# VectorE in program order from the first MLP on, and the state-space stage's inputs regrouped through device memory

## The chip, the cores and the metric

The kernel runs on one core of one Trainium2 chip, in one launch. The metric is device time in microseconds. Three runs of the kernel before gave 2471.07, 2461.07 and 2458.48 us, median 2461.07. Five engines work side by side: TensorE (PE; its weight loads are shown as PEld), VectorE (DVE), ScalarE (ACT), GpSimd (POOL) and SyncE (SP), which issues most of the DMAs. They meet through semaphores alone.

## The reference

A decoder trunk of two layers on one sequence of 256 tokens, model width 2048, all in float32. Layer 0 mixes tokens with stick-breaking attention, layer 1 with a diagonal state-space layer (S5) and a gated linear unit (GLU). Each layer ends with a squared-ReLU MLP of width 8192, and each of the four sub-layers is wrapped in the same way:

```
cond = silu(c)
mod = cond @ ada_w[i] + ada_b[i]              # 2048 -> 6 vectors of 2048
h = rmsnorm(x, g) * (1 + scale) + shift       # scale, shift: two of the six
x = x + gate * mixer(h)                       # gate: a third one
mlp(h)     = relu(h @ w1)**2 @ w2
s5(h):  u = h @ w_in;  state[t] = a * state[t-1] + B u[t]   (complex, 64 per group of 16 channels)
        z = gelu(C state + d * u);  y, g = split(z @ w_glu);  return y * sigmoid(g)
```

The weights are read once: 736 tiles of 512 KB for the matrix products and 384 tiles of 512 KB for `ada_w`.

## The kernel before

**Split products.** Each float32 product is made of three: a value is the sum of a rounded high part H and the remainder L, and TensorE sums L·H, H·L and H·H. A weight tile of 128x1024 therefore goes through four hands (`weights`, lines 126 to 134): SP issues its DMA into one of three buffers `w` (line 129), ScalarE copies it rounded to `wh` (line 131), VectorE subtracts to get `wl` (line 133), and TensorE multiplies with both (24 matmuls of some 256 columns on lines 160 to 162, or 12 of 512 columns on lines 146 to 148). `wh` and `wl` have three buffers each as well. So a `w` buffer is free for the next DMA when VectorE has made `wl` of it, and a `wl` buffer is free when TensorE is through with that tile.

**Ticks.** After each weight tile the program calls `tick`, which advances the products with `ada_w` by a fractional `rate` and then runs the functions that were booked for this tick with `at(delay, fn)`. The small stages of S5 and of the norms are interleaved with the weight tiles in this way.

**The products with `ada_w`.** They are sums over 2048 rows, one row block times one number per partition, on VectorE. A unit is one tile `adaw` of 128x1024 (four buffers; 32 units make one of the six vectors of a layer) and one VectorE instruction on line 356 (line 354 for the first of a sum), written straight after the load is issued. Sixteen units make one sum, for which there are three buffers (`adsums` two, `adacc` one); TensorE then adds it up over the partitions (`totals`, line 327) and frees it. The program asks for 0.42 units per weight tile in the first MLP (line 1236, from `between` on, after the first 16 tiles; 1.0 before), 0.35 in S5 (line 1248), and from the end of S5 as many as finish the last two vectors that the second MLP's input needs within 44 ticks (`pace(44, mid[-1])`, line 1122).

**Who sets the order.** `manual_schedule` on line 1190 keeps TensorE and GpSimd in the order in which the program writes their instructions. VectorE, ScalarE and SP follow a planner, which takes an instruction whenever its estimate says that it is ready, so a VectorE instruction written later can run earlier. Once planned, each engine and each DMA queue works its list strictly in order: an instruction that waits holds up all behind it.

**S5.** Eight weight groups of four tiles each give two blocks of 128 channels, 16 blocks in all, two ticks apart. For block `bi`, whose product is whole at tick T: `s5_windows` (T, VectorE then ScalarE) scales it to `u`; `s5_shuffle` (T+1) moves 32-channel strips, shifted by 0 to 3 tokens with stride 4, into other partitions with 16 matmuls against an identity (lines 1038 and 1039) and a ScalarE copy to `imc` (line 1040); `s5_operands` (T+1) and `s5_taps` (T+4) prepare operands on TensorE; `s5_states` (T+2) makes 8 matmuls with `imc` and then seven VectorE instructions (lines 1055 to 1063); `s5_outputs` (T+6) makes 44 matmuls, one VectorE instruction (line 1079) and a GELU. A float32 matmul of these shows as two records.

**The MLP.** `mlp` runs over four quarters of the 8192; `normal`, a square and `split` turn a pair of column blocks into the next operand `aH`, `aL`; `residual` adds a block to `x`, `square` adds its square to a running sum `sq`, `fold` scales it to the next sub-layer's `hH`, `hL`.

Of the kernel before, what the change touches and what calls it, by code (L numbers as in the profile page):

```python
# [8 lines left out]
F32 = mybir.dt.float32  # L9
# [7 lines left out]
P = 128  # L17
# [39 lines left out]
class Trunk:  # L57
    def __init__(self, ctx, tc, ins, out, dbg=None):
        self.ctx, self.tc, self.nc = ctx, tc, tc.nc
        self.i, self.out, self.dbg = ins, out, dbg or {}  # L60
        self.pers = ctx.enter_context(tc.tile_pool(name="pers", bufs=1))
        self.wp = ctx.enter_context(tc.tile_pool(name="wp", bufs=1))
        self.ps = ctx.enter_context(tc.tile_pool(name="ps", bufs=1, space=bass.MemoryType.PSUM))
        self.queue = []
        self.acc2 = self.wp.tile([P, 2, 512], F32, name="adacc", bufs=1)


# [67 lines left out]

    def gemm_rows(self, w2d, c0, aH, aL, k0, k1):
        nc = self.nc
        acc = self.accs()
        for t in range(k0 // 2, k1 // 2):
            r0 = 2 * t * P  # L140
            H, L = self.weights(w2d[r0:r0 + 2 * P, c0:c0 + 512].rearrange("(a p) b -> p a b", p=P), 2, 512)
            for kk in range(2):
                kb = 2 * t + kk
                for tb in range(2):
                    o, s = acc[:, tb], slice(tb * P, tb * P + P)
                    nc.tensor.matmul(o, aL(kb)[:, s], H[:, kk], start=(kb == k0), stop=False)  # L146
                    nc.tensor.matmul(o, aH(kb)[:, s], L[:, kk], start=False, stop=False)  # L147
                    nc.tensor.matmul(o, aH(kb)[:, s], H[:, kk], start=False, stop=(kb == k1 - 1))  # L148
            self.tick()
        return acc  # L150

    def cols_tile(self, acc, w2d, c0, t, aH, aL, k0=0, k1=NB):
        nc = self.nc
        r0, n = 4 * t * P, aH(0).shape[-1]
        H, L = self.weights(w2d[r0:r0 + 4 * P, c0:c0 + 256].rearrange("(a p) b -> p a b", p=P), 4, 256)
# [163 lines left out]
    def ada_dve(self, layer, groups):  # L319
        nc = self.nc  # L320
        st, rows = {}, 32 * len(groups)

        def totals(i0, accs):
            if i0 == 0:
                st["bank"] = self.ada_bank()
            for i, acc in enumerate(accs, i0):
                nc.tensor.matmul(st["bank"][32 * i:32 * i + 32], self.ones[:, 0:32], acc, start=True, stop=True)
# [13 lines left out]
        if self.sums is not None:  # L341
            for i in range(0, len(groups), 2):
                if self.turn % 3:
                    acc = self.sums.tile([P, 1024], F32, name="adsums", bufs=2)
                else:
                    acc = self.acc2.rearrange("p a b -> p (a b)")
                self.turn += 1
                accs += [acc[:, :512], acc[:, 512:]]
                vec, g = groups[i]
                for k in range(NB):  # L350
                    wt = self.ada_load(layer, vec, g, k, wide=True).rearrange("p a b -> p (a b)")
                    c = self.cond[:, k:k + 1]
                    if k == 0:
                        nc.vector.tensor_scalar(acc, wt, c, None, op0=OP.mult)
                    else:
                        nc.vector.scalar_tensor_tensor(acc, wt, c, acc, op0=OP.mult, op1=OP.add)  # L356
                    yield
            self.later(2, totals, 0, accs)
        for i, (vec, g) in enumerate(groups if not accs else []):
# [12 lines left out]
            self.later(2, totals, i, accs[i:])  # L372
        self.later(2, evict)
        self.later(3, finish)

    def ada_vec(self, layer, vec, on_pe=False):
        g = self.pending[layer, vec] = self.ada(layer, [(vec, g) for g in range(4)], on_pe)
# [61 lines left out]
    def square(self, sq, kb):  # L439
        nc = self.nc  # L440
        if kb == 0:
            nc.scalar.activation(sq, self.xT[:, kb], AF.Square)
        else:
            t = self.wp.tile([P, S], F32, name="sqt", bufs=2)
            nc.scalar.activation(t, self.xT[:, kb], AF.Square)
            nc.vector.tensor_tensor(sq, sq, t, op=OP.add)

    def new_sq(self):
        return self.wp.tile([P, S], F32, name="sqa", bufs=1)
# [52 lines left out]
    def mlp(ctx, self, layer, nxt=None, last=False, between=None):  # L502
# [9 lines left out]
        for q in range(4):  # L512
# [12 lines left out]
            for g in range(8):  # L525
# [376 lines left out]
    def s5_open(self, sp):  # L902
        g_ = self.nc.gpsimd
        self.sE = sp.tile([P, 2, 4, 4, 2, 16], F32, name="E")
        self.sCA = [sp.tile([P, 2, 4, 4, 2, 16], F32, name="CA%d" % k) for k in range(3)]
        self.sKL = [sp.tile([P, 3, 4, 2, 16], F32, name="KL%d" % k) for k in range(3)]
        self.simc = [sp.tile([P, 4, 65], F32, name="imc%d" % k) for k in range(3)]
        self.sU = [sp.tile([P, 4 + S + 1], F32, name="u%d" % k) for k in range(3)]
        self.sM = [sp.tile([P, 2, 4, 64], F32, name="M%d" % k) for k in range(2)]
        self.sP = [sp.tile([P, 224], F32, name="taps%d" % k) for k in range(2)]  # L910
        for t in [self.sE] + self.sP + self.sM + self.sCA + [u[:, 0:4] for u in self.sU]:
            g_.memset(t, 0.0)
        self.sS = {}

# [108 lines left out]
            nc.tensor.transpose(pk[:, tau * P - P:tau * P], self.sP[bi % 2][:, o:o + P], self.ident)  # L1023
        nc.scalar.activation(self.sKL[bi % 3].rearrange("p t q a e -> p (t q a e)"), pk[:, :3 * P], AF.Copy)

    def s5_windows(self, bi, acc):
        nc = self.nc
        uw = self.sU[bi % 3]
        nc.vector.tensor_tensor(uw[:, 4:], acc[:, :S + 1], self.rms, op=OP.mult)
        nc.scalar.activation(uw[:, 4:4 + S], uw[:, 4:4 + S], AF.Identity, bias=uw[:, 4 + S:])  # L1030

    def s5_shuffle(self, bi):
        nc = self.nc
        uw, imc = self.sU[bi % 3], self.simc[bi % 3]
        pi = self.mp()
        for q in range(4):
            for j in range(4):
                nc.tensor.matmul(pi[32 * j:32 * j + 32, 65 * q:65 * q + 65], self.ident[:, 32 * q:32 * q + 32],  # L1038
                                 uw[:, 4 - j:4 - j + 257:4], start=True, stop=True)
        nc.scalar.activation(imc.rearrange("p q k -> p (q k)"), pi[:, :4 * 65], AF.Copy)  # L1040

    def s5_states(self, sp, bi):
        nc, s5 = self.nc, self.s5
# [20 lines left out]

    def s5_outputs(self, sp, bi):
        nc = self.nc
        u, St = self.sU[bi % 3][:, 4:4 + S], self.sS.pop((bi, "R")).rearrange("p c (q k) -> p c q k", q=4)
# [11 lines left out]
        nc.vector.scalar_tensor_tensor(u.rearrange("p (k i) -> p i k", i=4), u.rearrange("p (k i) -> p i k", i=4),  # L1079
                                       self.dcol[:, bi:bi + 1], py[:, 0:S].rearrange("p (i k) -> p i k", i=4),  # L1080
                                       op0=OP.mult, op1=OP.add)
        nc.scalar.activation(self.z[:, bi], u, AF.Gelu_apprx_tanh)
        if not self.split_z:
            self.sdone.add(bi)
        else:
# [2 lines left out]
    def s5_mixer(self, mid):  # L1088
# [11 lines left out]
        for gi in range(8):  # L1100
# [82 lines left out]
    def run(self):  # L1183
# [100 lines left out]
```

## Time and profile before

| what | value |
|---|---|
| runs, us | 2471.07, 2461.07, 2458.48 (median 2461.07) |
| profiled execution, us | 2467.97 |
| its span, first to last instruction, us | 2466.1 |
| mean granted clock of TensorE | 0.989 |
| TensorE matmuls busy | 2365.1 us, 96% |
| VectorE busy | 1795.4 us, 73% |
| ScalarE busy | 1212.7 us, 49% |
| moved by DMA | 627.09 MB, 254 GB/s over the span |

The profile is of one execution. Busy times of matmuls overlap and their ends are modelled, so a busy TensorE can still lose time between tiles; the time that a weight tile takes, a stretch of the span divided by the tiles in it, is the steadier measure. Stages by the span's clock: attention to 455 us, first MLP to 1311, S5 and its change-over to the GLU to 1520, GLU to 1725, second MLP to the end. An engine's idle time is put down to the last semaphore that it waited for.

### The profile page before, as it was taken

How to read it: one execution, taken by the hardware profiler on the slowest of the kernel's cores; microseconds unless marked ns; L12 is line 12 of the kernel's file. 1: busy time of each engine (PE TensorE's matmuls, PEld its weight loads, DVE VectorE, ACT ScalarE, POOL GpSimd, SP SyncE). 2: the span in 40 equal slices, each digit the busy share in tenths (PEclk: the TensorE clock that was granted, in tenths of full speed). 3: DMA queues.
4: the chain of work that ended last, by engine and by line, in shares of the span. 5: the costliest groups of instructions: out<-in, count | busy, mean ns of one | idle time of the engine just before them, and what ended most of it. 6: DMA issues, size and time to landing. Idle time of an engine off the chain costs nothing.

```text
span 2466.1 us, 45235 instructions
## 1 busy us (share of the span) xinstructions
PE 2365.1 (96%) x18355; PEld 2160.4 (88%) x18355; DVE 1795.4 (73%) x2223; ACT 1212.7 (49%) x1814; POOL 316.6 (13%) x340
## 2 busy tenths in 40 slices
PE   7999999999998999889999999989999999999999
PEld 4777789899988899889998998989998998998987
DVE  5789999999778767875786668888744554555554
ACT  4534875346334335435546776434554543543543
POOL 0000110001056545445300000000000000000000
PEclk9999999999999999999999999999999999999999
DMA  9888899999999967997798544999856555556565
GB/s 341 302 299 306 288 308 320 322 303 294 310 310 315 300 207 230 309 299 219 259 316 276 174 154 159 314 329 314 281 175 192 184 186 190 175 179 193 180 195 164
DMA packets 416773, 627.09 MB, mean 254 GB/s; under 512 B 19858, under 2 KB 282420, under 8 KB 414260
## 3 DMA queue, kind: packets, MB, share of 16 engines
q1 hardware_dynamic: 411968, 606.16, 74.8%
q0 software_dynamic: 3968, 17.83, 2.2%
q8 instruction: 144, 2.36, 0.4%
q14 instruction: 65, 0.53, 0.1%
q10 hardware_dynamic: 628, 0.21, 0.0%
HBM read 607.34 MB, written 16.78 MB: 253 GB/s over the span
## 4 chain that ended last, share of the span: by engine, by line
PE 44%; DMA 6%; DVE 5%; issue 3%; ACT 0%; SPq 0%; DVEq 0%; ACTq 0%
PE acc L160 9%; PE acc L162 8%; PE acc L161 8%; DMA adaw<-in_ada_w 5%; PE acc L146 5%; PE acc L148 5%; PE acc L147 5%; DVE wl L133 2%; PE mp L1053 1%; DVE adsums L356 1%; PE mp L1078 1%; PE mp L1038 1%; PE mp L1015 1%; DVE xT L435 1%; DMA w<-in_s_w_glu 0%
## 5 line engine op out<-in xcount | busy, mean ns | idle before, releaser
L131 ACT ACTIVATE wh<-w 128x1024 fp32r<-128x1024 f32 x736 | 777.5, 1058 | 1030.9 <-PE acc L162 364.6
L133 DVE TENSOR_TENSOR wl<-w,wh 128x1024 fp32r<-128x1024 f32 x736 | 922.6, 1255 | 436.9 <-ACT wh L131 434.3
L160 PE MATMUL acc<-hH,wl 128*128 128x258 f32 (+1 forms) x2816 | 808.4, 287 | 28.4 <-DVE wl L133 26.1
L162 PE MATMUL acc<-hH,wh 128*128 128x258 f32 (+1 forms) x2816 | 799.2, 284 | 0.0
L161 PE MATMUL acc<-hL,wh 128*128 128x258 f32 (+1 forms) x2816 | 797.8, 283 | 0.2 <-DVE hL L123 0.2
L160 PEld LDWEIGHTS acc<-hH,wl 128*128 128x128 f32 x2816 | 535.8, 190 | 44.3 <-DVE wl L133 33.6
L161 PEld LDWEIGHTS acc<-hL,wh 128*128 128x128 f32 x2816 | 536.3, 190 | 0.6 <-DVE hL L123 0.4
L162 PEld LDWEIGHTS acc<-hH,wh 128*128 128x128 f32 x2816 | 534.8, 190 | 0.0
L160 PE MATMUL acc<-aH,wl 128*128 128x256 f32 x1024 | 294.3, 287 | 26.4 <-DVE wl L133 25.5
L161 PE MATMUL acc<-aL,wh 128*128 128x256 f32 x1024 | 289.5, 283 | 0.0
L162 PE MATMUL acc<-aH,wh 128*128 128x256 f32 x1024 | 289.4, 283 | 0.0
L356 DVE SCALAR_TENSOR_TENSOR adsums<-adaw,cond,adsums 128x1024 f32<-128x1024 f32 x150 | 199.1, 1328 | 53.6 <-DMA adaw<-in_ada_w 53.0
L160 PEld LDWEIGHTS acc<-aH,wl 128*128 128x128 f32 x1024 | 194.3, 190 | 34.1 <-DVE wl L133 33.7
L146 PE MATMUL acc<-wh,aL 128*128 128x512 f32 x512 | 202.2, 395 | 0.0
L148 PE MATMUL acc<-wh,aH 128*128 128x512 f32 x512 | 202.1, 395 | 0.0
L147 PE MATMUL acc<-wl,aH 128*128 128x512 f32 x512 | 202.0, 395 | 0.0
L161 PEld LDWEIGHTS acc<-aL,wh 128*128 128x128 f32 x1024 | 194.4, 190 | 0.0
L162 PEld LDWEIGHTS acc<-aH,wh 128*128 128x128 f32 x1024 | 194.2, 190 | 0.0
L370 DVE SCALAR_TENSOR_TENSOR adacc<-adaw,cond,adacc 128x512 f32<-128x512 f32 x240 | 179.2, 750 | 3.1 <-DMA adaw<-in_ada_w 1.3
L146 PE MATMUL acc<-wh,hL 128*128 128x512 f32 x384 | 157.5, 410 | 5.8 <-ACT wh L131 3.1
L147 PE MATMUL acc<-wl,hH 128*128 128x512 f32 x384 | 153.8, 401 | 3.3 <-DVE wl L133 3.2
L148 PE MATMUL acc<-wh,hH 128*128 128x512 f32 x384 | 152.9, 398 | 0.0
(311 smaller groups left out, 2751.0 us busy)
## 6 DMA issues: line engine op xcount, KB each, us to landing
w<-in_mlp_w SPq DMA_DIRECT2D x512, 512.0 KB, 4.0
adaw<-in_ada_w SPq DMA_DIRECT2D x384, 512.0 KB, 6.0
w<-in_sb_w_in SPq DMA_DIRECT2D x96, 512.0 KB, 5.2
w<-in_s_w_glu SPq DMA_DIRECT2D x64, 512.0 KB, 5.4
w<-in_sb_w_out SPq DMA_DIRECT2D x32, 512.0 KB, 5.7
w<-in_s_w_in SPq DMA_DIRECT2D x32, 512.0 KB, 4.8
pw<-W POOLq DMA_DIRECT2D x8, 1024.0 KB, 6.5
W<-pw SPq DMA_DIRECT2D x8, 1024.0 KB, 7.7
```

The lines of the kernel that those rows point to most:

```text
L131: nc.scalar.activation(h, w, AF.Copy)
L133: nc.vector.tensor_tensor(l, w, h.bitcast(F32), op=OP.subtract)
L146: nc.tensor.matmul(o, aL(kb)[:, s], H[:, kk], start=(kb == k0), stop=False)
L147: nc.tensor.matmul(o, aH(kb)[:, s], L[:, kk], start=False, stop=False)
L148: nc.tensor.matmul(o, aH(kb)[:, s], H[:, kk], start=False, stop=(kb == k1 - 1))
L160: nc.tensor.matmul(o, L[:, kk, s], aH(kb), start=(kb == k0), stop=False)
L161: nc.tensor.matmul(o, H[:, kk, s], aL(kb), start=False, stop=False)
L162: nc.tensor.matmul(o, H[:, kk, s], aH(kb), start=False, stop=(kb == k1 - 1))
L356: nc.vector.scalar_tensor_tensor(acc, wt, c, acc, op0=OP.mult, op1=OP.add)
L370: nc.vector.scalar_tensor_tensor(acc, wt[:, kk], c, acc, op0=OP.mult, op1=OP.add)
L435: nc.vector.scalar_tensor_tensor(x, y, self.mod[layer][:, vec * 16 + kb:vec * 16 + kb + 1], x, op0=OP.mult, op1=OP.add)
L1015: nc.tensor.transpose(pe[:, q * P:q * P + P], E[:, c, q].rearrange("p j a e -> p (j a e)"), self.ident)
```

## The change

Four things are changed, all from the end of attention on except where named.

VectorE joins TensorE and GpSimd in `manual_schedule`, so its instructions run in the order in which the program writes them. SP and ScalarE stay with the planner.

`weights` takes its tiles from a list written ahead (`tiles`): DMA, `wh` and `wl` of a tile are written two tiles before its matmuls. The number of buffers is the same.

Some VectorE instructions are written later: a product with `ada_w` two units after its load (`overdue(2)`), and the sum of squares and `aL` of the MLP one tick later (`behind`).

In S5, `s5_windows` and `s5_shuffle` are replaced. `s5_inputs` (T) writes `u` with the four token phases side by side and stores it (128 KB) to device memory on ScalarE's DMA queue; `s5_regroup` (T+1) reads it back into `imc` with four DMAs of 32 KB on SP, in runs of 64 numbers (256 bytes). `s5_states` moves from T+2 to T+3. `s5_outputs` reads `u` in the new order.

```diff
+    def tiles(self):
...
     def weights(self, src, a, b):
+        if self.seq is None:
+            return self.fetch(src, a, b)
+        while len(self.ready) < 3 and self.seq:
+            nxt, a_, b_ = self.seq.pop(0)
+            self.ready.append((str(nxt), self.fetch(nxt, a_, b_)))
+        name, pair = self.ready.pop(0)
+        assert name == str(src), (name, str(src))
+        return pair
...
         def totals(i0, accs):
+            self.overdue(0)
...
                     wt = self.ada_load(layer, vec, g, k, wide=True).rearrange("p a b -> p (a b)")
-                    c = self.cond[:, k:k + 1]
-                    if k == 0:
-                        nc.vector.tensor_scalar(acc, wt, c, None, op0=OP.mult)
-                    else:
-                        nc.vector.scalar_tensor_tensor(acc, wt, c, acc, op0=OP.mult, op1=OP.add)
+                    self.due.append((self.ada_product, acc, wt, k))
+                    self.overdue(2)
                     yield
...
+    def overdue(self, n):
+        while len(self.due) > n:
+            fn, *args = self.due.pop(0)
+            fn(*args)
...
-            nc.vector.tensor_tensor(sq, sq, t, op=OP.add)
+            self.behind(nc.vector.tensor_tensor, sq, sq, t, OP.add)
+
+    def behind(self, fn, *args):
+        if self.seq is None:
+            fn(*args)
+        else:
+            self.at(1, fn, *args)
...
-                self.split(aH[:, 2 * g:2 * g + 2], aL[:, 2 * g:2 * g + 2], r)
+                nc.scalar.activation(aH[:, 2 * g:2 * g + 2], r, AF.Copy)
+                self.behind(nc.vector.tensor_tensor, aL[:, 2 * g:2 * g + 2], r, aH[:, 2 * g:2 * g + 2].bitcast(F32), OP.subtract)
...
-    def s5_windows(self, bi, acc):
...
-    def s5_shuffle(self, bi):
...
+    def s5_inputs(self, sp, bi, acc):
+        nc = self.nc
+        uw, u = sp.tile([P, S + 1], F32, name="uw", bufs=1), self.sU[bi % 3]
+        nc.vector.tensor_tensor(uw, acc[:, :S + 1], self.rms, op=OP.mult)
+        nc.scalar.activation(u.rearrange("p (i k) -> p i k", i=4), uw[:, :S].rearrange("p (k i) -> p i k", i=4), AF.Identity, bias=uw[:, S:])
+        nc.scalar.dma_start(self.um[bi], u)
+
+    def s5_regroup(self, bi):
+        nc, imc = self.nc, self.simc[bi % 3]
+        src = self.um[bi].rearrange("(q p) (i k) -> i p q k", q=4, i=4)
+        for j in range(4):
+            o = 1 if j else 0
+            nc.sync.dma_start(imc[32 * j:32 * j + 32, :, o:o + 64], src[(4 - j) % 4])
...
-                self.at(t, self.s5_windows, bi, acc[:, b])
+                self.at(t, self.s5_inputs, sp, bi, acc[:, b])
                 self.at(t + 1, self.s5_operands, sp, bi)
-                self.at(t + 1, self.s5_shuffle, bi)
-                self.at(t + 2, self.s5_states, sp, bi)
+                self.at(t + 1, self.s5_regroup, bi)
+                self.at(t + 3, self.s5_states, sp, bi)
...
         self.attention(sets, gates[0])
         self.dump("x1")
+        self.ctx.enter_context(self.tc.manual_schedule(engines={mybir.EngineType.PE, mybir.EngineType.Pool, mybir.EngineType.DVE}))
+        self.seq = list(self.tiles())
```

## Rows read from the trace of the kernel before

**Rows 1.** The page's first part: busy us, share of the span, instructions.
```profile
PE 2365.1 (96%) x18355; PEld 2160.4 (88%) x18355; DVE 1795.4 (73%) x2223; ACT 1212.7 (49%) x1814; POOL 316.6 (13%) x340
```

**Rows 2.** The chain that ended last, by engine.
```profile
PE 44%; DMA 6%; DVE 5%; issue 3%; ACT 0%; SPq 0%; DVEq 0%; ACTq 0%
```

**Rows 3.** TensorE's waits, and SP's: us in total, times, longest.
```profile
PE acc L160 <- DVE wl L133: 57.4, 49, 3.7
...
SPq L129 <- DVE wl L133: 1459.4, 655, 6.9
```

**Rows 4.** Stages: us, busy us of each engine, clock, DMA share, GB/s.
```profile
545.00:855.00 310.00, 288.34 (x2317) 281.68 (x2316) 261.38 (x270) 137.74 (x174) 119.64 (x116) 0.98 0.92 306
855.00:950.00 95.00, 92.76 (x766) 92.65 (x766) 59.01 (x60) 42.67 (x48) 32.61 (x36) 0.98 0.69 210
...
1311.00:1520.00 209.00, 204.09 (x3279) 188.85 (x3283) 141.88 (x200) 149.58 (x312) 0.69 (x4) 0.99 0.55 176
1520.00:1660.00 140.00, 126.09 (x1167) 120.80 (x1167) 123.89 (x143) 57.22 (x74) 0.00 (x0) 0.99 0.92 315
...
1725.00:2400.00 675.00, 673.16 (x4393) 615.32 (x4394) 370.83 (x346) 323.42 (x386) 0.00 (x0) 1.00 0.62 194
```

**Rows 5.** Stages, weight tiles alone (line 133): us, DVE busy (tiles), clock, DMA.
```profile
545.00:855.00 310.00, 125.72 (x95) 0.98 0.92 306
855.00:950.00 95.00, 42.98 (x33) 0.98 0.69 210
1100.00:1205.00 105.00, 48.27 (x37) 1.00 0.71 218
545.00:1205.00 660.00, 276.86 (x209) 0.99 0.85 276
1205.00:1311.00 106.00, 41.38 (x34) 1.00 0.92 308
1520.00:1660.00 140.00, 48.78 (x40) 0.99 0.92 315
1660.00:1725.00 65.00, 24.82 (x21) 1.00 0.90 306
```

**Rows 6.** Stages, products with adaw alone: us, PE, PEld, DVE busy (products), DMA.
```profile
545.00:855.00 310.00, 0.00 (x0) 0.00 (x0) 94.79 (x70) 0.98 0.92 306
545.00:1205.00 660.00, 0.00 (x0) 0.00 (x0) 140.91 (x102) 0.99 0.85 276
1205.00:1311.00 106.00, 0.00 (x0) 0.00 (x0) 38.57 (x31) 1.00 0.92 308
1311.00:1520.00 209.00, 0.00 (x0) 0.00 (x0) 1.27 (x1) 0.99 0.55 176
1520.00:1660.00 140.00, 0.00 (x0) 0.00 (x0) 60.53 (x49) 0.99 0.92 315
1660.00:1725.00 65.00, 0.00 (x0) 0.00 (x0) 20.00 (x16) 1.00 0.90 306
```

**Rows 7.** VectorE's waits for the tiles of ada_w.
```profile
DVE adsums L356 <- DMA adaw<-in_ada_w: 53.0, 48, 3.6
...
DVE adacc L356 <- DMA adaw<-in_ada_w: 17.6, 17, 2.9
```

**Rows 8.** The chain between 1400 and 1415 us: start, us, what.
```profile
1401.39 1.06 PE mp L1038 x32
...
1413.62 1.06 PE mp L1038 x32
```

**Rows 9.** The page's DMA issues: count, KB each, median us to landing.
```profile
T<-rot SPq DMA_DIRECT2D x16, 384.0 KB, 3.6
...
C<-in_s_c_re POOLq DMA_DIRECT2D x16, 64.0 KB, 6.6
...
vecs<-in_ada_b ACTq DMA_DIRECT2D x2, 48.0 KB, 1.8
```

**Rows 10.** VectorE between 1520 and 1660 us: shapes, count, busy us, mean ns.
```profile
L356 DVE SCALAR_TENSOR_TENSOR adsums<-adaw,cond,adsums 128x1024 f32<-128x1024 f32 x30 | 38.4, 1281 | 10.8 <-DMA adaw<-in_ada_w 10.6
```

More of the change, by code (lines that the diff above doesn't have):

```diff
@@ L63, in __init__ @@
         self.ps = ctx.enter_context(tc.tile_pool(name="ps", bufs=1, space=bass.MemoryType.PSUM))
-        self.queue = []
+        self.queue, self.seq, self.ready, self.due = [], None, [], []
         self.acc2 = self.wp.tile([P, 2, 512], F32, name="adacc", bufs=1)
@@ L123, in split, with fetch @@
         self.nc.vector.tensor_tensor(lo, src, hi.bitcast(F32), op=OP.subtract)
-    def weights(self, src, a, b):
+    def tiles(self):
+        i = self.i
+        rows = lambda w, c0, k0=0, k1=NB: [(w[2 * t * P:2 * t * P + 2 * P, c0:c0 + 512], 2, 512) for t in range(k0 // 2, k1 // 2)]
+        cols = lambda w, c0, k0=0, k1=NB: [(w[4 * t * P:4 * t * P + 4 * P, c0:c0 + 256], 4, 256) for t in range(k0 // 4, k1 // 4)]
+        for layer in range(2):
+            w1, w2 = i["mlp_w1"][layer], i["mlp_w2"][layer]
+            if layer:
+                w, v = i["s5_w_in"][0], i["s5_w_glu"][0]
+                for g in range(8):
+                    yield from cols(w, g * 256)
+                yield from cols(v, D, 0, 12) + cols(v, 0, 0, 12) + cols(v, D, 12) + cols(v, 0, 12)
+                for g in range(1, 8):
+                    yield from cols(v, D + g * 256) + cols(v, g * 256)
+            for q in range(4):
+                if q == 0 and layer == 0:
+                    for k in (0, 8):
+                        for g in range(8):
+                            yield from cols(w1, g * 256, k, k + 8)
+                else:
+                    for g in range(8):
+                        yield from cols(w1, q * 2048 + g * 256)
+                part = w2[q * 2048:q * 2048 + 2048]
+                for g in range(4 if layer else 8):
+                    yield from rows(part, g * 512) if layer else cols(part, g * 256)
+    def weights(self, src, a, b):
+        if self.seq is None:
[6 more added lines that the diff above has]
+        return pair
+    def fetch(self, src, a, b):
+        src = src.rearrange("(a p) b -> p a b", p=P)
         nc = self.nc
@@ L140, in gemm_rows @@
             r0 = 2 * t * P
-            H, L = self.weights(w2d[r0:r0 + 2 * P, c0:c0 + 512].rearrange("(a p) b -> p a b", p=P), 2, 512)
+            H, L = self.weights(w2d[r0:r0 + 2 * P, c0:c0 + 512], 2, 512)
             for kk in range(2):
@@ L154, in cols_tile @@
         r0, n = 4 * t * P, aH(0).shape[-1]
-        H, L = self.weights(w2d[r0:r0 + 4 * P, c0:c0 + 256].rearrange("(a p) b -> p a b", p=P), 4, 256)
+        H, L = self.weights(w2d[r0:r0 + 4 * P, c0:c0 + 256], 4, 256)
         for kk in range(4):
@@ L374, in ada_dve, with ada_product @@
         self.later(3, finish)
+    def ada_product(self, acc, wt, k):
+        c = self.cond[:, k:k + 1]
+        if k == 0:
+            self.nc.vector.tensor_scalar(acc, wt, c, None, op0=OP.mult)
+        else:
+            self.nc.vector.scalar_tensor_tensor(acc, wt, c, acc, op0=OP.mult, op1=OP.add)
+    def overdue(self, n):
+        while len(self.due) > n:
+            fn, *args = self.due.pop(0)
+            fn(*args)
     def ada_vec(self, layer, vec, on_pe=False):
@@ L445, in square @@
             nc.scalar.activation(t, self.xT[:, kb], AF.Square)
-            nc.vector.tensor_tensor(sq, sq, t, op=OP.add)
+            self.behind(nc.vector.tensor_tensor, sq, sq, t, OP.add)
+    def behind(self, fn, *args):
+        if self.seq is None:
+            fn(*args)
+        else:
+            self.at(1, fn, *args)
     def new_sq(self):
@@ L907, in s5_open @@
         self.simc = [sp.tile([P, 4, 65], F32, name="imc%d" % k) for k in range(3)]
-        self.sU = [sp.tile([P, 4 + S + 1], F32, name="u%d" % k) for k in range(3)]
+        self.sU = [sp.tile([P, S], F32, name="u%d" % k) for k in range(3)]
+        self.um = [self.dram.tile([P, S], F32, name="um%d" % bi) for bi in range(16)]
         self.sM = [sp.tile([P, 2, 4, 64], F32, name="M%d" % k) for k in range(2)]
         self.sP = [sp.tile([P, 224], F32, name="taps%d" % k) for k in range(2)]
-        for t in [self.sE] + self.sP + self.sM + self.sCA + [u[:, 0:4] for u in self.sU]:
+        for t in [self.sE] + self.sP + self.sM + self.sCA + self.simc:
             g_.memset(t, 0.0)
@@ L1024, in s5_taps @@
         nc.scalar.activation(self.sKL[bi % 3].rearrange("p t q a e -> p (t q a e)"), pk[:, :3 * P], AF.Copy)
-    def s5_windows(self, bi, acc):
+    def s5_inputs(self, sp, bi, acc):
         nc = self.nc
-        uw = self.sU[bi % 3]
-        nc.vector.tensor_tensor(uw[:, 4:], acc[:, :S + 1], self.rms, op=OP.mult)
-        nc.scalar.activation(uw[:, 4:4 + S], uw[:, 4:4 + S], AF.Identity, bias=uw[:, 4 + S:])
-    def s5_shuffle(self, bi):
[L1033 to L1040, printed above, removed]
+        uw, u = sp.tile([P, S + 1], F32, name="uw", bufs=1), self.sU[bi % 3]
[8 more added lines that the diff above has]
+            nc.sync.dma_start(imc[32 * j:32 * j + 32, :, o:o + 64], src[(4 - j) % 4])
     def s5_states(self, sp, bi):
@@ L1066, in s5_outputs @@
         nc = self.nc
-        u, St = self.sU[bi % 3][:, 4:4 + S], self.sS.pop((bi, "R")).rearrange("p c (q k) -> p c q k", q=4)
+        u, St = self.sU[bi % 3], self.sS.pop((bi, "R")).rearrange("p c (q k) -> p c q k", q=4)
         CA, KL, imc = self.sCA[bi % 3], self.sKL[bi % 3], self.simc[bi % 3]
@@ L1078, in s5_outputs @@
                     nc.tensor.matmul(o, lhs.rearrange("p a e -> p (a e)"), rhs, start=(c == 0), stop=(c == (2 if tau else 1)))
[L1079 to L1082, printed above, removed]
+        nc.vector.scalar_tensor_tensor(u, u, self.dcol[:, bi:bi + 1], py[:, 0:S], op0=OP.mult, op1=OP.add)
+        nc.scalar.activation(self.z[:, bi].rearrange("p (k i) -> p i k", i=4), u.rearrange("p (i k) -> p i k", i=4), AF.Gelu_apprx_tanh)
         if not self.split_z:
```

## The prediction

> **What bounds the kernel now.** I read the page's busy shares first: TensorE is busy 96% of the span, no other engine over 75% [rows 1]. In the chain of waits TensorE has 44%, DMA 6% and VectorE 5% [rows 2]; the reader is to see that the rest is cut into pieces too small to be listed, and that what interrupts TensorE is data. The waits say which: 57.4 us before the first matmul of a tile, always for the remainder `wl` of VectorE [rows 3]. SP in turn waits 1459.4 us for `wl` [rows 3]: three `w` buffers make a ring (DMA, ScalarE, VectorE, DMA again), and whoever delays `wl` delays the DMA three tiles on.
>
> Then the stages, by time per weight tile. Between 545 and 855 us a tile takes 310/95 = 3.26 us, between 855 and 950 95/33 = 2.88, between 1100 and 1205 105/37 = 2.84 [rows 5]. The difference is in the products with `ada_w`: 70 of them in the first stretch, 0.74 per tile [rows 6]; the second has a DMA share of 0.69 against 0.92 and VectorE busy 59 of 95 us against 261 of 310 [rows 4]. In all there are 102 products for 209 tiles between 545 and 1205 [rows 5, 6], 0.49 per tile, and the program asks for 0.42. So the planner runs products ahead in bursts until the buffers for sums are full, then pauses; in a burst the DMA engines are nearly full and VectorE waits in place for tiles of `ada_w`, 53.0 + 17.6 us in all [rows 7]. In S5 TensorE is busy 204 of 209 us; in the second MLP 673 of 675 [rows 4].
>
> **The change part by part.**
>
> *First MLP, even pacing.* VectorE in written order can't run a product ahead of its tick, and with four `adaw` buffers no load either. The bursts become 0.42 per tile throughout. Bounds for a tile: below, 2.86, the mean of the two stretches without products; above, the straight line from there to 3.26 at 0.74, which gives 3.09 at 0.42. I take 2.97, a little under the middle, since the DMA share at that density lies between 0.69 and 0.92 at about 0.83 and the wait for `ada_w` goes: four products lie between a buffer's release and its next use. Before: 660/209 = 3.16. Gain 209 x 0.19 = 40 us (bounds 15 and 63). Between 1205 and 1311 a tile takes 106/34 = 3.12 with 31 products [rows 5, 6]; at 3.0 this gives back 4. Against it: in the last quarter each of 8 groups has two remainders of `fold` for which VectorE now waits in place for ScalarE; two tiles of lead cover most of it, and I charge 0.5 us a group, 4 in all (0 to 1.28, one product [rows 10], a group). Zero together.
>
> *`weights` two tiles ahead, `behind`, `overdue`.* With VectorE in order, `wl` of tile t+2 stands before anything that waits for tile t, so evictions don't hold it up. I cost them at nothing: TensorE has two tiles, 5.7 us, in hand. If that cover is gone, a group's end shows as a wait for `wl`.
>
> *S5, TensorE.* The identity products take 1.06 us in a block [rows 8], 16 blocks: 17 us off an engine that sets this stage. A block's period is 1413.62 - 1401.39 = 12.23 us now and 11.17 after. The ScalarE copy goes, an issue comes; nothing.
>
> *S5, VectorE.* It was busy 141.88 us [rows 4] with a single product [rows 6]; written order puts 0.35 x 33 = 12 there, 11 more at 1.28 us [rows 10], so 156 of the 192 us left. Hidden behind TensorE; 14 us if not.
>
> *S5, the detour.* `u` is stored at T and must be back before `s5_states` at T+3: two ticks of 5.6 us and the tile of T+3, 14 us, less 2 for the two instructions that make `u` and their queues (an estimate: one product is 1.28 [rows 10]). The trace has no such round trip. From below: 1.8 us for 48 KB on ScalarE's queue and 3.6 for 384 KB on SP, 5.4. From above: 6.6 twice, 13.2, as for the 64 KB of `s5_c_re` in the same 256-byte runs [rows 9]. I take the low end, as the weight DMAs leave S5 at a share of 0.55 [rows 4], and SP's and ScalarE's queues are those of its two rows. At the high end a block is 1 us late and the 17 us are gone. SP waits with the weight DMAs behind it until the store has landed; with 5.6 us a tick the ring has room. At the change-over, where the DMA fills up again, I charge 2 us (0 to 8).
>
> The Trainium skill ("DMA: Bandwidth & Descriptors", Specifications, and Anatomy of one DMA — SWDGE (gpsimd) path) puts a DMA at about 2.0 us fixed plus bytes at 436 GB/s and warns of transfers below 512 bytes. Its fixed part would make the round trip an estimated 4.4 us and leave the 17 us whole; the 256-byte rows took 6.6 us for 64 KB [rows 9], three times what it gives, in a fuller stretch, so the warning is what this trace bears out.
>
> *GLU.* Here even pacing costs. By the code 25 units are done between `ready` and the end of S5 (32 x 0.42 + 33 x 0.35) and 71 of the 96 of the last three vectors are left for 44 ticks, 1.64 per tile. Before, products had been run ahead, and between 1520 and 1660 there were 49 for 40 tiles, 1.23, at 140/40 = 3.50 us a tile [rows 5, 6]. At 1.64 VectorE needs 48.78/40 + 1.64 x 1.28 + 0.36 = 3.68 us a tile (0.36: the rest of its 123.89 us [rows 4]). The DMAs bring 2.64 x 0.524 = 1.38 MB a tile; 315 GB/s at a share of 0.92 [rows 4] make 342 when full, 4.0 us. I take 4.0 (bounds 3.68 and 4.4, the latter at 315 GB/s). Some 38 of the 44 ticks fall after 1520: 38 x 0.5 = +19 (7 to 34). The six before it gain some 10 products, beside S5's last blocks: +6 (0 to 13). The last 21 tiles took 65/21 = 3.10 with 16 products of a vector not yet due [rows 5, 6], and lose these: -3. GLU: +22 (4 to 47).
>
> *Second MLP.* No product is run ahead into it; TensorE is full [rows 4], VectorE at 370.83 of 675. Nothing.
>
> **Sum.** -40 + 0 - 17 + 2 + 22 = -33 us. Against the profiled execution's 2467.97 (span 2466.1) this is 2435. That execution is 6.9 us over the median of the three runs, 2461.07, so I forecast 2428 for the median.
>
> **The rivals.**
>
> *The GLU pays more than the MLP gains* (slower). One mechanism: a product can no longer be done before its tick, so the 71 units fall on 44 ticks whose DMAs and VectorE are both full, and a late `ada_w` tile now holds VectorE, and `wl` behind it. At 4.5 us a tile: 38 + 13 - 3 = +48; with the MLP on the straight line, -15; S5 -17, change-over +8. Sum +24, 2485. It decides from about 4.3 us a tile there together with 3.05 in the MLP. For it: the DMA share of 0.92 and VectorE's 124 of 140 us now [rows 4]. Against: the MLP's pauses show that evenness pays there.
>
> *The regrouped inputs come late.* S5 gains nothing, change-over +8: -33 + 17 + 6 = -10, 2451. For it the 6.6 us [rows 9]; against it the half-empty DMA engines.
>
> *Evenness pays in full.* A tile of the MLP takes 2.87 and the GLU is bound by VectorE alone at 3.68: -61 - 17 + 2 + 7 = -69, 2392. For it the 2.84 and 2.88 [rows 5]; against it GpSimd's own DMAs in those stretches and the ring of three buffers.
>
> *The planner moves them all the same.* If products on VectorE still came in bursts, only S5's 17 us would go: 2446. The code speaks against it; it has its part in the chance of the regrouping case.
>
> **How the numbers follow.** Forecast 0.48 (its own range 2405 to 2450), slower GLU 0.22, late or unmoved 0.14, full gain 0.16. A measurement of this kernel can tell about 0.5%, 12 us, from no change: faster means under 2449, slower over 2473. Faster: 0.41 of the forecast, 0.16, and 0.06 of the third; same: 0.04 + 0.04 + 0.05; slower: 0.18 + 0.03 + 0.03. That is 0.63, 0.13, 0.24. The terms at their better bounds give -67 - 17 + 0 + 4 = -80, at their worse -15 + 6 + 0 + 8 + 47 = +46, so 2381 to 2507; leaving a tenth at each end gives 2388 to 2486.
>
> **What would show it.** Products between 850 and 950 and between 1100 and 1205 where there were none, and 0.4 per tile throughout; tiles at 2.9 to 3.0 us in the first MLP; the wait for `ada_w` on VectorE near zero there. S5's blocks 11.2 us apart, with TensorE not waiting for the DMA of `imc`. Some 1.6 products and 4 us a tile in the GLU's first 44 ticks, at a DMA share of 0.95 or more. The prediction is wrong if the MLP's tile stays at 3.1 or more, if S5's period stays at 12 us, or if the GLU takes no longer than before.

## The result and the profile after

The changed kernel took 2530.76 us (median of 4 runs, 2523.02 to 2534.80) beside 2462.55 us for the kernel before (median of 4): over all runs 1.0269 times as long, 95% interval 1.0229 to 1.0308. Forecast were 2428 us, range 2388 to 2486, so the sign was missed, the value by 103 us and the range by 45. The profiled execution took 2523.02 us, its span 2521.1. In the changed file the loads of `w` are line 165, `wl` line 169, the columns' matmuls 196 to 198, the loads of `ada_w` 304, their products 413 and 415, `totals` 364, the store of `u` 1085, its reads 1092 and the states' matmuls 1105.

The page: engines [rows 1], the chain by engine [rows 2], and the new transfers (count, KB each, median us from issue to landing).

```profile
PE 2375.2 (94%) x17843; PEld 2170.6 (86%) x17843; DVE 1804.2 (72%) x2223; ACT 1215.9 (48%) x1798; POOL 320.6 (13%) x340
...
PE 36%; DMA 7%; DVE 6%; ACT 3%; issue 2%; SPq 1%; ACTq 0%; DVEq 0%
...
um<-u ACTq DMA_DIRECT2D x16, 128.0 KB, 4.8
imc<-um SPq DMA_DIRECT2D x64, 32.0 KB, 1.8
```

TensorE has 512 matmul records fewer and is yet busy 10 us longer; its part of the chain fell from 44% to 36%. Where the time went is seen best from the ends of `wl`, by the number of the weight tile. This table is worked out from the traces: us between the end of `wl` of the first and the last tile named.

| tiles | before | changed | lag 1 | no lag | planner | detour only | window |
|---|---|---|---|---|---|---|---|
| 120-144, first MLP | 84.5 | 77.4 | 76.1 | 76.2 | 80.2 | 83.5 | 79.7 |
| 144-160, first MLP | 47.0 | 64.0 | 65.7 | 65.9 | 50.2 | 47.4 | 45.8 |
| 160-384, first MLP | 709.3 | 693.0 | 678.2 | 673.7 | 712.4 | 708.7 | 680.4 |
| 384-416, S5 | 176.4 | 171.2 | 171.7 | 167.1 | 165.0 | 163.8 | 166.2 |
| 416-424, change-over | 51.6 | 65.7 | 63.5 | 60.4 | 49.4 | 52.6 | 51.1 |
| 424-464, GLU | 136.4 | 181.7 | 168.4 | 145.2 | 132.3 | 134.4 | 150.7 |
| 464-480, GLU | 48.4 | 52.3 | 52.3 | 52.3 | 52.7 | 47.7 | 51.6 |
| 480-735, second MLP | 736.3 | 740.4 | 739.3 | 738.6 | 738.2 | 736.3 | 738.4 |

(The last five columns are the experiments e13, e5, e1, e10 and e16.) Each column is one execution, and a second one of the kernel without the lag (e14) took 680.2 us in tiles 160 to 384 and 64.9 at the change-over, so a few us between columns mean little. Of the 55 us between the two spans, 14 came at the change-over and 45 in 40 tiles of the GLU; 8 behind them; the first MLP gave back 6 net, S5 5.

The stretches of [rows 5], weight tiles alone (line 169): us, DVE busy (tiles), clock, DMA share, GB/s.

```profile
545.00:1205.00 660.00, 280.68 (x210) 0.98 0.82 266
1520.00:1660.00 140.00, 36.65 (x30) 0.89 0.87 280
1660.00:1725.00 65.00, 17.13 (x14) 0.89 0.77 255
```

The stretches of [rows 6], products with `adaw` alone: us, PE, PEld, DVE busy (products), clock, DMA share, GB/s.

```profile
855.00:950.00 95.00, 0.00 (x0) 0.00 (x0) 18.11 (x13) 0.98 0.86 278
1100.00:1205.00 105.00, 0.00 (x0) 0.00 (x0) 22.89 (x16) 1.00 0.88 289
1520.00:1660.00 140.00, 0.00 (x0) 0.00 (x0) 58.36 (x47) 0.89 0.87 280
```

Pacing did become even: 13 and 16 products where there had been none. But in 140 us of the GLU there are 30 tiles with 47 products, where there had been 40 with 49. And neither resource that the prediction feared is full there. All engines [rows 4] (us, PE, PEld, DVE, ACT, POOL busy, clock, DMA share, GB/s):

```profile
1311.00:1520.00 209.00, 193.16 (x2760) 181.11 (x2760) 157.07 (x209) 143.54 (x279) 0.00 (x0) 0.93 0.68 221
1520.00:1660.00 140.00, 112.15 (x953) 107.03 (x953) 106.83 (x114) 44.22 (x57) 0.00 (x0) 0.89 0.87 280
```

DMA share 0.87, VectorE 107 of 140 us (76%): less than before, when more was done. Something holds both. VectorE's waits for tiles of `ada_w` in products of line 415 over the whole span [rows 7] (us, times, longest):

```profile
DVE adsums L415 <- DMA adaw<-in_ada_w: 1.3, 1, 1.3
...
DVE adacc L415 <- DMA adaw<-in_ada_w: 0.8, 2, 0.5
```

So it is not a late `ada_w` tile that holds VectorE. What SP's DMA queue waited for (us, times, longest) in the GLU, 1520 to 1700 us, in the kernel before:

```profile
SPq L129 <- DVE wl L133: 76.0, 34, 6.9
SPq L268 <- DVE adsums L356: 17.8, 14, 3.1
SPq L268 <- DVE adacc L356: 11.5, 10, 2.3
```

and in the changed one:

```profile
SPq L304 <- DVE adsums L415: 63.9, 27, 6.0
SPq L304 <- DVE adacc L415: 41.9, 23, 5.9
SPq L165 <- DVE wl L169: 24.5, 7, 11.3
```

SP stood 105.8 us before loads of `ada_w` whose buffer was not free, against 29.3; only 24.5 us for `wl`, against 76.0. So the ring of `w` seldom lacked a free buffer, and by this reading, which e4 tests, the weight DMAs that would have filled it stood on SP behind an `ada_w` load.

TensorE's waits [rows 3]:

```profile
PE acc L196 <- DVE wl L169: 67.2, 45, 4.9
PE mp L364 <- DVE adsums L415: 19.0, 5, 9.6
...
PE mp L1105 <- DMA imc<-um: 5.6, 5, 1.5
PE mp L364 <- DVE adacc L415: 5.5, 2, 4.4
```

The sums over partitions are new among them: 24.5 us where the kernel before had none listed. The longest stands at the change-over; the chain there (start, us, what):

```profile
1500.84 0.61 DVE w L1108
...
1505.48 1.14 DVE wl L169
1506.61 1.19 DVE adsums L415
1507.81 0.40 DVE u L1131
...
1510.84 1.29 DVE adsums L415
1512.13 0.04 issue
1512.18 1.95 PE mp L364 x4
```

`totals` flushes the lagged products (`overdue(0)`) and TensorE, in order, waits until VectorE has worked off states, `wl`, products and `u`. TensorE alone there (us, PE busy, clock, DMA share, GB/s):

```profile
1500.00:1505.00 5.00, 2.62 (x18) 1.00 0.55 188
1505.00:1510.00 5.00, 0.00 (x0) 0.75 0.72 203
1510.00:1515.00 5.00, 2.13 (x5) 0.50 0.86 278
1515.00:1520.00 5.00, 5.00 (x25) 0.50 0.79 275
```

During this stop its granted clock fell to the lower level (0.50, 1.2 GHz) and was still there from 1515 to 1520 us, when it was busy throughout; in the next two stretches of 5 us it was 0.88 and 1.00.

### The profile page after: what moved, and what is told of

Same layout as the page of the kernel before. It is cut to its first block, busy times and chain, and to the rows that moved or that the text cites. A ratio compares the mean times of both kernels' runs of the same rounds, so it can differ in the third digit from the quotient of the medians.

```text
span 2521.1 us, 44243 instructions
## 1 busy us (share of the span) xinstructions
PE 2375.2 (94%) x17843; PEld 2170.6 (86%) x17843; DVE 1804.2 (72%) x2223; ACT 1215.9 (48%) x1798; POOL 320.6 (13%) x340
## 4 chain that ended last, share of the span: by engine, by line
PE 36%; DMA 7%; DVE 6%; ACT 3%; issue 2%; SPq 1%; ACTq 0%; DVEq 0%
PE acc L196 7%; PE acc L198 6%; PE acc L197 6%; PE acc L183 5%; PE acc L182 5%; PE acc L184 5%; DMA w<-in_s_w_glu 3%; DVE wl L169 2%; DMA w<-in_mlp_w 2%; ACT wh L167 1%; DMA um<-u 1%; DVE adsums L415 1%; DMA w<-in_s_w_in 1%; DVE adacc L415 1%; PE mp L1105 1%
## 5 line engine op out<-in xcount | busy, mean ns | idle before, releaser
L196 PE MATMUL acc<-hH,wl 128*128 128x258 f32 (+1 forms) x2816 | 821.4, 292 | 52.5 <-DVE wl L169 50.3
L197 PE MATMUL acc<-hL,wh 128*128 128x258 f32 (+1 forms) x2816 | 810.2, 288 | 4.6 <-DVE hL L536 4.5
L198 PE MATMUL acc<-hH,wh 128*128 128x258 f32 (+1 forms) x2816 | 810.6, 288 | 0.0
L196 PEld LDWEIGHTS acc<-hH,wl 128*128 128x128 f32 x2816 | 548.9, 195 | 67.9 <-DVE wl L169 55.9
L197 PEld LDWEIGHTS acc<-hL,wh 128*128 128x128 f32 x2816 | 549.8, 195 | 5.1 <-issue 4.7
L198 PEld LDWEIGHTS acc<-hH,wh 128*128 128x128 f32 x2816 | 547.7, 194 | 0.0
```

## The experiments

Theory after this reading: the lag of two units (`overdue(2)`) costs the time, through SP's queue and through the flushed sums. Rivals: written order as such, the detour, or the backlog of products that nobody ran ahead.

**e1, e2: one part each.** e1 takes VectorE out of the written order, e2 takes out the detour.

The edit of e1 (e2 puts back the S5 code of the kernel before):

```diff
-        self.ctx.enter_context(self.tc.manual_schedule(engines={mybir.EngineType.PE, mybir.EngineType.Pool, mybir.EngineType.DVE}))
+        self.ctx.enter_context(self.tc.manual_schedule(engines={mybir.EngineType.PE, mybir.EngineType.Pool}))
```

> The changed kernel with VectorE left to the planner; the list of weight tiles, overdue, behind and the detour of S5 stay. Theory (the written order of VectorE costs: no product before its tick, so the GLU carries 1.64 per tile): the GLU's 40 tiles from 424 to 464 come back from 182 us to about 136 to 145, and the total to 2440 to 2460, a little under the kernel before for S5. Rival (the detour, or the list written ahead, costs): the total stays above 2500.

> The change without its S5 part: identity products as before, VectorE in written order. Theory: the GLU stays at about 182 us for its tiles 424 to 464, S5's blocks go back from 10.9 to 12.2 us, and the total is 2530 to 2550. Rival (the detour's DMAs and SP's wait for them upset the change-over and the GLU): the GLU comes back to under 150 us and the total to under 2480.

e1: 2458.13 us, ratio 0.9971 (0.9954 to 0.9989); e2: 2564.95, 1.0399 (1.0370 to 1.0429). So the written order, with the lag of two in it, loses the time (e5 parts the two), and the detour does not: under written order it saves 2565 - 2531 = 34 us. e2 lies above the 2530 to 2550 of its theory: its blocks in S5 are 14.3 us apart (median of the 15 intervals), where 12.2 was expected, and TensorE waits for `u` before every block but one:

```profile
PE mp L1091 <- ACT u L1083: 33.4, 15, 4.2
```

**e3, e4: the two ways, each alone.** e3 books `totals` four units behind the last load and no longer flushes; e4 issues the loads of three vectors on GpSimd's queue.

```diff
-            self.overdue(0)
+            if self.flushing or not self.queue:
+                self.overdue(0)
...
-            self.later(2, totals, 0, accs)
+            self.later(4, totals, 0, accs)
...
```

```diff
-            self.nc.sync.dma_start(wt, w[t * P:t * P + P, c0:c0 + 1024].rearrange("p (a b) -> p a b", a=2))
+            q = self.nc.gpsimd if layer == 1 and vec in (2, 3, 4) else self.nc.sync
+            q.dma_start(wt, w[t * P:t * P + P, c0:c0 + 1024].rearrange("p (a b) -> p a b", a=2))
```

> The changed kernel, with the sums' matmuls (totals) booked four units after the last load in place of two, so that TensorE does not reach them while VectorE still has the last products to make. Theory (TensorE waits in its own order for those products, 19 us in the profile, and the clock drops after each stop): these waits vanish and the total falls by 15 to 25 us, to about 2505 to 2515; the GLU's tiles stay at 4.5 us. Rival (VectorE is late anyway, and the wait moves to the weight tiles): the total stays within 8 us.

> The changed kernel, with the ada_w loads of the last three vectors before the second MLP (96 tiles of 512 KB) issued on GpSimd's DMA queue in place of SP's. Bytes, buffers and order on VectorE are the same; only weight DMAs no longer stand behind loads that wait for a buffer. Theory (SP is held: 106 us of its time between 1520 and 1700 is a wait for VectorE to free an ada_w buffer): a GLU tile falls from 4.5 us to about 4.0 or less, where DMA and VectorE set it, the total to about 2500 to 2510. Rival (the DMA engines are full, whoever issues): a GLU tile stays at 4.4 to 4.6 and the total at 2525 to 2535.

e3: 2511.18, 1.0174 (1.0137 to 1.0211), TensorE's waits for sums nearly gone (1.8 + 1.0 us, where 24.5 were). e4: 2513.10, 1.0192 (1.0158 to 1.0226), tiles 424 to 464 in 160 us in place of 182. In e4 SP no longer stands before `ada_w` from 1520 to 1700:

```profile
SPq L165 <- DVE wl L169: 142.3, 41, 14.3
...
SPq L305 <- DVE adacc L416: 0.7, 1, 0.7
```

Each is real, since the runs of both (2500 to 2516, 2509 to 2521) lie below all of the changed kernel's; each explains some 20 us. e4 is 3 us above its theory's range. The clock did not drop after each stop before a sum, as the expectation of e3 has it: in the changed kernel it was 0.50 to 0.55 in the 5 us after four of the seven stops, and 1.00 after the other three.

**e5: no lag.** The product is written straight after its load.

```diff
-                    self.overdue(2)
+                    self.overdue(0)
```

> The changed kernel with a product written at the unit of its load in place of two units later. Theory (SP is held because with four buffers and a lag of two units a load waits for a product written only two units before it): SP's wait for ada_w buffers between 1500 and 1700 falls from 106 us to under 50, a GLU tile from 4.5 to about 4.0, and VectorE now waits for some ada_w DMAs; total 2500 to 2515. Rival (DMA bandwidth or VectorE's load set the GLU): tile and total unchanged within 8 us.

2464.97 (2457.91 to 2473.71, 10 runs), 1.0001 (0.9986 to 1.0016): the whole loss is gone, 66 us by one digit, far more than either way had shown alone and better than the theory's 2500 to 2515. SP's wait for buffers of `ada_w` fell less than the theory had it, to 63.2 us and not under 50. SP from 1520 to 1700:

```profile
SPq L165 <- DVE wl L169: 63.7, 27, 9.0
SPq L304 <- DVE adsums L415: 42.3, 26, 3.4
SPq L304 <- DVE adacc L415: 20.9, 16, 2.4
```

**e6, e7: the backlog.** Rates of 0.61 in the first MLP and S5, with the lag; in e7 also the later sums of e3.

```diff
-            self.rate = 0.42
+            self.rate = 0.61
...
-        self.rate = 0.35
+        self.rate = 0.61
```

> The changed kernel with 0.61 units per tick in the first MLP and in S5 (before 0.42 and 0.35), so that about 27 units instead of 71 are left for the 44 ticks of the GLU: 0.61 everywhere. Theory (the GLU pays because written order puts 1.64 units per tile there): the GLU's 40 tiles 424 to 464 go from 182 us to about 120 to 125, the first MLP loses 10 to 25 us and S5 up to 10; total 2490 to 2505. Rival (something else of the written order slows the GLU, S5's last blocks or the wait for ScalarE): the GLU stays above 160 us and the total above 2520.

> Even rates of 0.61 and the sums' matmuls two units later, together. Theory: both gains add, as the one takes a wait in TensorE's order and the other a load on VectorE and SP: 2470 to 2485, near the kernel before. Rival (both act on the same lateness of VectorE): no better than the even rates alone within 8 us.

2494.85, 1.0123 (1.0096 to 1.0151), and 2484.78, 1.0086 (1.0068 to 1.0104). In e6 tiles 424 to 464 took 118 us, but S5 took 195 (24 more, where up to 10 was expected) and tiles 160 to 384 took 713. In e7 the later sums add 10 us, half of the 20 that they gave alone in e3. Less backlog helps a kernel with the lag; without the lag the GLU with the whole backlog takes 9 us more there than the kernel before (145.2 against 136.4).

**e8: the planner with GpSimd's queue.** e1 and e4 together.

> VectorE left to the planner (as in the run with the planner, 2458), and the ada_w loads of the last three vectors on GpSimd's DMA queue. Theory (a load that waits for its buffer holds weight DMAs behind it on SP in any order of VectorE; SP waited 29 us for ada_w buffers between 1500 and 1700 there): the GLU's 40 tiles gain 5 to 15 us and the total falls to 2440 to 2455. Rival (with the planner SP's holds lie beside other waits): within 6 us of 2458.

2474.50, 1.0053 (1.0030 to 1.0077), slower than e1 and above its theory's 2440 to 2455: GpSimd's queue has a price of its own. e4 seems to have paid it too, as its tiles 160 to 416 took 16 us more than those of the changed kernel.

**e9, e15, e14: do the two ways make up the lag?** e9 is e3 and e4 together; e15 is e5 with e4's queue. e14 is, in spite of its name, the kernel of e5 once more, one run beside them.

> The changed kernel, still with the lag of two units, but with both of its suspected costs taken away at once: the ada_w loads of vectors 2, 3 and 4 of layer 1 on GpSimd's DMA queue (a load that waits for a buffer no longer stands before weight DMAs on SP) and the sums over partitions four units later without a flush (no backlog of products that TensorE waits for). Alone these gave 2513 and 2511 against 2531. Theory (the lag costs by these two ways and by no other): close to the kernel without the lag, 2465 to 2480. Rival (the two are independent and there is a third): 2531 - 18 - 20 = 2493 or more.

> The changed kernel without the lag, with the ada_w loads of vectors 2, 3 and 4 of layer 1 on GpSimd's queue. With the lag, these loads there and the sums later, the kernel took 2497, 32 above the kernel without the lag. Theory (GpSimd's queue costs some 16 us by itself, as it did under the planner, 2474 against 2458; the two suspected ways and this price account for the lag but for some 16 us): 2476 to 2486. Rival (GpSimd's queue is free, and the lag has a third way worth 30 us): 2460 to 2470.

> Replaced by the next run if not needed: the changed kernel without the lag, one look, on the same chip as the others of this call. Both theories: 2458 to 2474, as before.

e9: 2496.63, 1.0111 (1.0081 to 1.0142), above its theory's 2465 to 2480. e15: 2486.59, 1.0097 (1.0068 to 1.0127). e14: 2474.96. e15 lies 0.6 us above its theory's range, and the rival is out. So GpSimd's queue costs 2487 - 2465 = 22 us by the medians, 12 by the single run of e14. With that queue on both sides, the lag costs 2497 - 2487 = 10 us by the medians once sums come late. But the two intervals overlap, the two profiled executions took 2485.07 and 2485.25 us, and tiles 424 to 464 took 150.6 us in e9 and 149.5 in e15. The two ways therefore hold at least 56 of its 66 us, if the queue's price is the same with the lag; a third way is not shown.

The Trainium skill ("Trainium Kernel Development and Optimization", Key Constraints) says that DMAs issued from several engines share the same 16 DMA engines, and that this only saves a sequencer's issue time. e15 agrees, as nothing was won there (22 us lost, though SP had stood 63.2 us before these loads in e5); e4 differs, since a load that waits for its buffer holds its queue for far longer than an issue takes (63.9 us in 27 waits, 2.4 each, in the changed kernel, where the 64 reads of `imc` took 0.43 us to issue, the median).

**e13: by degrees?** One unit of lag.

> The changed kernel with a product written one unit after its load instead of two (none gave 2465, two 2531). Theory (four buffers: with a lag of n a load waits for a product written 4 - n units before it, and each unit of lag takes away the same cover): between them, near the middle, 2485 to 2510, SP's wait for a buffer of ada_w between 69 and 106 us from 1480 to 1700. Rival (a threshold: three units of cover are enough, two are not): 2462 to 2475. A second rival (any lag costs, because the sums are then flushed late for TensorE): 2520 or more.

2493.07, 1.0114 (1.0099 to 1.0129), between the two. SP from 1520 to 1700:

```profile
SPq L304 <- DVE adsums L415: 50.8, 25, 3.9
SPq L165 <- DVE wl L169: 34.6, 10, 9.5
SPq L304 <- DVE adacc L415: 33.8, 21, 4.0
```

SP stands before `ada_w` for 63.2, 84.6 and 105.8 us at a lag of 0, 1 and 2, 21 us a unit; the time goes 2465, 2493, 2531. These 180 us hold other tiles in each run; between the ends of tiles 424 and 464 the waits are 66.3, 84.6 and 104.2 us, which says the same. Between 0 and 2 no threshold shows.

**e10: the detour alone,** in the kernel before.

> The kernel before with the S5 detour alone: store and reads in place of the identity products, s5_states a tick later, everything else and the planner as before. Theory (the detour is worth its identity products, 17 us of the S5 stage, and nothing in the list or the delays of the change helps the planner): 2445 to 2452. Rival (the regrouped inputs or SP's wait for the store eat it): 2458 or more, as with the whole change under the planner.

2454.30, 0.9960 (0.9944 to 0.9976), and S5 in 163.8 us for 176.4: 12 us in place of the 17 forecast, short of the theory's range (2445 to 2452) and better than its rival (2458 or more).

**e11, e12, e16: where written order pays.** All without the lag. e11 begins it after the tables of S5 are written, e12 also ends it at the end of S5, e16 begins it one product later still, at tile 160. The edit of e16, beside `overdue(0)` and without the `manual_schedule` line that e1 changes:

```diff
+            if q == 0 and between:
+                self.order = ExitStack()
+                self.order.enter_context(self.tc.manual_schedule(engines={mybir.EngineType.PE, mybir.EngineType.Pool, mybir.EngineType.DVE}))
             if q == 3 and nxt:
...
+        self.order.close()
         self.split_z = True
         self.pace(44, mid[-1])
```

> The changed kernel without the lag, with VectorE's written order beginning only after the tables of S5 are written (after the first half sums of the MLP) instead of at the end of attention. Without the lag tiles 144 to 160 still took 66 us where the planner took 50, all with the tables in VectorE's list. Theory (that stretch loses because VectorE waits in place inside the tables and folds): 2465 - 15 = 2450, range 2444 to 2458. Rival (the planner only shifts the same work, and it is paid behind): 2461 to 2470.

> As the last, and VectorE goes back to the planner at the end of S5, so that the GLU is planned. Theory (the GLU loses under written order because its products come on fixed ticks and folds are waited for in place; the planner took 136 us from tile 424 to 464 and the order without the lag 145): another 10 us, 2440, range 2432 to 2452. Rival (what the GLU costs is the backlog of products that no one ran ahead, which the planner can't give back there): 2447 to 2458, no better than the last.

> The kernel with the written order in a window (no lag, planner again from the end of S5), with the window opened some 20 tiles later, after the first quarter's first product: tiles 144 to 160, which took 60 us with the order and 47 to 50 with the planner, are planned. Theory (that stretch loses only by the order inside it): 2454 - 12 = 2442, range 2436 to 2450. Rival (the work that the planner pushes out of that stretch is paid behind it, as in the planner's tiles 160 to 192): 2452 to 2460.

e11: 2458.01, 0.9977 (0.9962 to 0.9992), at the edge of its theory's range; tiles 144 to 160 still took 61 us, so beginning after the tables is not enough. e12: 2454.41, 0.9956 (0.9928 to 0.9984); the planner gains 6 us at the change-over and nothing in the GLU proper (147.8 for 147.0), so the rival is right there. e16: 2443.53 (2440.44 to 2447.04), 0.9911 (0.9891 to 0.9930), as its theory had it, and faster than both kernels. Some of the rival shows too: of the 14 us won against e12 in tiles 144 to 160, 3 go in tiles 120 to 144 and 5 in 160 to 384. Tiles 144 to 160, all engines, in the changed kernel:

```profile
540.60:604.60 64.00, 52.06 (x389) 49.73 (x387) 53.74 (x97) 31.77 (x45) 0.00 (x0) 0.95 0.64 210
```

and in e16, with the same work asked for by the program, and 51 VectorE instructions in place of 97 in the stretch:

```profile
546.00:591.80 45.80, 45.65 (x377) 45.44 (x378) 41.94 (x51) 30.27 (x44) 0.00 (x0) 1.00 0.87 293
```

## Why the prediction was wrong

**The step that failed** is the one on "`weights` two tiles ahead, `behind`, `overdue`", "I cost them at nothing", with the words it leaned on, "four products lie between a buffer's release and its next use". The product of unit n - 4 frees the buffer for the load of unit n; at a lag of two it is written after the load of unit n - 2, so two units lie between, not four. At 1.64 units a tile that is 1.2 tiles. The diff showed it, and the prediction had named the queue (SP) but counted only `wl` and the store of `u` on it. Measured in place of nothing: 66 us (e5), by degrees (e13).

**GLU, +22.** It came to +14 in tiles 416 to 424, +45 in 424 to 464, +4 in 464 to 480: 63, outside its bounds of 4 to 47. A tile took 181.7/40 = 4.54 us; 4.0 was forecast from a full DMA. The price of the slower-GLU rival (4.5) was right, its mechanism was not: VectorE waited 2 us for `ada_w`, and the DMA engines were not full (a share of 0.90, where e5 reached 0.99). The products with `adaw` in tiles 424 to 464, in the changed kernel:

```profile
1534.50:1716.20 181.70, 0.00 (x0) 0.00 (x0) 74.90 (x60) 0.88 0.90 291
```

and in e5:

```profile
1507.80:1653.00 145.20, 0.00 (x0) 0.00 (x0) 72.45 (x58) 0.98 0.99 347
```

The same 40 tiles with 60 and 58 products, 1.5 a tile and not 1.64. Without the lag the stage is what the prediction said it would be, bound by a full DMA: 347 GB/s (342 assumed), 3.63 us a tile. The term then has the size forecast too: +9, +9 and +4 in the same three groups of tiles, 22. With the lag nearly the same bytes came at 291 GB/s.

**First MLP, -40.** Tiles 120 to 384 gave 6, and between 545 and 1205 us a tile took 660/210 = 3.14 us, over the 3.1 that the prediction had named as a sign of being wrong. The mechanism holds: without the lag tiles 160 to 384 took 673.7 us for 709.3, 36 less, 3.01 a tile (2.97 forecast, 3.17 before). The lag took 19 of it (693.0; 13 by the second profile, e14), and 9.5 of it came back with the later sums of e3 (683.5). Another 17 went in tiles 144 to 160, which the prediction had only as part of an average: VectorE in order works tables, half sums and folds in place there, and the clock was 0.95. Which of these holds it was not separated. e16 takes 45.8 us there, by leaving that stretch to the planner.

**S5, -17.** Where nothing disturbs it, the period is as forecast, 11.18 us between these two starts:

```profile
1435.02 1.97 PE mp L1105 x16
...
1446.20 1.73 PE mp L1105 x16
```

Over all 15 intervals between blocks the median fell from 12.25 to 11.02 us, but three in a row took 12.5 to 14.2 in the changed kernel, and its last 25.1 for 12.2, as the flushed sums stand there. Over the stage only 5 came, 12 in e10. The detour was quick, 4.8 + 1.8 = 6.6 us by the medians, near the low end of 5.4 to 13.2. TensorE waited 5.6 us for `imc`, SP 88.9 us for the store between 1311 and 1520:

```profile
SPq L1092 <- DMA um<-u: 88.9, 16, 9.3
```

Which of these became time was not separated. VectorE was busy 157.07 us between 1311 and 1520, as forecast (156). That under written order the detour is worth 34 and not 17 was missed: the identity products, in order, made TensorE wait for `u` (e2).

**Totals** were not in the sum at all: 24.5 us of TensorE's waits, 20 us of the time (e3). **Second MLP, 0:** 4.

**Even without the lag** the kernel only equals the one before: -36 in tiles 160 to 384, -8 in the first 24 and -9 in S5, against +19 in tiles 144 to 160 and +24 from the change-over on. That adds up to -10 in the profiled execution, the fastest of its 10; the medians are equal, and the runs of this kernel spread over 16 us.

**Open:** whether the lag has a third way (10 us by the medians, within the noise), why GpSimd's queue costs 12 to 22, and what holds tiles 144 to 160 in order.

## What to carry to other kernels

A load that waits for its buffer holds what stands behind it on its queue; count the work between a buffer's release and its next use as buffers less lag, in the busiest stage, and look at SP's waits by tile. Fixing VectorE's order paid here in a stage with a steady beat (tiles 160 to 384) and lost where a burst of small work had to be fitted in (144 to 160), so try it by stage: the same change, without the lag and in a window, went from 2.7% slower to 0.9% faster.

## What was unexpected of the hardware

A store of 128 KB to device memory landed 4.8 us after its issue, and 32 KB came back in runs of 256 bytes in 1.8 us, against 6.6 us for the 64 KB of the nearest row [rows 9], which stands on GpSimd's queue. So short runs, which the prediction saw borne out as slow by that row, were not slow here. The trace of the kernel before also has 8 KB on ScalarE's queue in 4.9 us, beside the 1.8 us for 48 KB that the prediction took. The Trainium skill ("DMA: Bandwidth & Descriptors", Anatomy of one DMA — SWDGE (gpsimd) path) would put the two at an estimated 2.3 and 2.1 us by its 2.0 us and 436 GB/s, a fit for GpSimd's path; the read is a little faster than that, the store twice as slow, and the measurement decides.

The granted clock of TensorE was 0.89 from 1520 to 1725 us, 0.99 to 1.00 before [rows 5], with TensorE less busy. In tiles 424 to 464 of the changed kernel TensorE stopped seven times for 3.5 to 4.9 us, six times for `wl` and once for a sum, and the clock was 0.50 to 0.69 in the 5 us after each; e5 has no stop of that length there. All engines over these tiles, in the changed kernel and in e5:

```profile
1534.50:1716.20 181.70, 140.24 (x981) 131.94 (x980) 131.39 (x136) 55.39 (x70) 0.00 (x0) 0.88 0.90 291
1507.80:1653.00 145.20, 126.38 (x984) 119.26 (x984) 128.68 (x135) 55.88 (x70) 0.00 (x0) 0.98 0.99 347
```

The same work kept TensorE busy 13.9 us longer; the other 22.6 of the 36.5 us between the two are idle. Whether the slower matmuls alone cost time was not measured apart.
